# The up projections of the second model's feed-forward with seven half-size products for each two

## The chip, the core and the metric

The kernel runs on one core of a Trainium2 chip. Its time is the device time of one execution, in microseconds (us). The engines are TensorE (PE; its weight loads are a row of their own, PEld), VectorE (DVE), ScalarE (ACT), GpSimd (POOL), and SyncE (SP), which here issues DMAs. SBUF is the memory that all of them read; PSUM takes what TensorE writes.

## The reference

The program computes two models one after the other on 512 tokens of width 1024: a block with attention, a state-space mixer, memory attention and a mixture of single-neuron experts, and then two layers of a hybrid model with three branches. All is in float32. The change touches the feed-forward at the end of each of these two layers:

```python
f = jnp.square(jax.nn.relu(rmsnorm(h, norm2_g) @ w_up)) @ w_down    # w_up: 1024 x 4096, w_down: 4096 x 1024
return h + f
```

## The kernel before

Activations lie transposed: `h` is eight tiles of 128 features x 512 tokens. A weight matrix is stored so that one DMA of 512 KB brings 128 output columns with all 1024 inputs, a tile of 128 x 8 x 128. To keep float32 accuracy, every operand X of a large product is split into H, X rounded to the engine's fast float32 form, and L, the rest X - H: `split` lets ScalarE write H and VectorE write L. A product of 1024 inputs is then eight times three matmuls, wH·xH, wH·xL and wL·xH (`mm3`, lines 170 to 172), each with its own weight load of 128 x 128 and a moving operand of 512 columns.

`weight` (line 155) takes a raw buffer `wr` (three of them), issues the load on SP, and splits into `wH`, `wL` (two each). So a product's weights are split while the one before runs, and a load starts when a raw buffer has been read.

`ffn` first multiplies the eight tiles of `h` by the norm's gain and splits them (`gain_split`), while `rstd_tile` forms the tokens' scale `rs`: squares, sums over features by TensorE (line 185), an inverse square root in small VectorE steps (lines 131 to 142), a transpose (191) and a spread over partitions (196). The scale comes in only after the product. In each of four groups come eight up products (VectorE: max(ps, 0)·rs, line 1963; ScalarE: the square, line 1964; then a split, tag `y`) and eight down products that add into `h`. Just ahead of `ffn`, `run` has eight output products that add into the same `h` (line 1949).

Nobody wrote the order of instructions down: the framework plans it. It walks the program, gives each engine a list by priority and by its own guess of durations, and puts waits where a tile or a buffer has to be ready. Each engine then goes through its list in order, so an instruction that waits holds all behind it on its engine.

Of the kernel before, what the change touches and what calls it, by code (L numbers as in the profile page):

```python
# [11 lines left out]
F32 = mybir.dt.float32  # L12
F32R = mybir.dt.float32r
I32 = mybir.dt.int32
U32 = mybir.dt.uint32
AF = mybir.ActivationFunctionType
OP = mybir.AluOpType
# [4 lines left out]
P = 128  # L22
T = 512
EPS = 1e-6
# [25 lines left out]
class Builder:  # L50
# [5 lines left out]
    def __init__(self, tc, d, ctx):  # L56
        self.tc, self.nc, self.d = tc, tc.nc, d
        self.n = 0
        self.home = {}

        self.rush = False
        self.turn, self.three = 0, True
        self.sb = ctx.enter_context(tc.tile_pool(name="sb", bufs=1))
        self.pp = ctx.enter_context(tc.tile_pool(name="pp", bufs=1, space=PSUM))
        self.dr = ctx.enter_context(tc.tile_pool(name="dr", bufs=1, space=DRAM))
        self.consts()
# [94 lines left out]
            self.split(r, H, L)  # L161
        return H, L

    def mm3(self, ps, wH, wL, xs, start=True, stop=True):

        nc = self.nc
        n = len(xs)
        for k, (xH, xL) in enumerate(xs):
            s, e = start and k == 0, stop and k == n - 1
            nc.tensor.matmul(ps, wH[:, k], xH, start=s, stop=False)  # L170
            nc.tensor.matmul(ps, wH[:, k], xL, start=False, stop=False)  # L171
            nc.tensor.matmul(ps, wL[:, k], xH, start=False, stop=e)  # L172

    def gemm(self, ap, xs, n=T, ps=None):

        H, L = ap if isinstance(ap, tuple) else self.weight(ap, len(xs))
        ps = self.psg()[:, :n] if ps is None else ps
        self.mm3(ps, H, L, xs)
        return ps


    def colsum(self, ps, acc, n=T):
# [43 lines left out]

    def rstd_tile(self, srcs, width, eps=EPS, out=None):

        acc = self.sumsq(srcs)
        cs, ps = self.pss(), self.pss()  # L230
        self.colsum(cs, acc)
        r = self.small([P, T // P])
        self.rsqrt(r, cs[:, :T // P], 1.0 / width, eps)
        self.rowbc(ps, r)
        out = acc if out is None else out
        self.nc.scalar.copy(out, ps)
        return out
# [663 lines left out]
def vcol(vec, base, n):  # L901
    return [vec[:, base + k:base + k + 1] for k in range(n)]
# [344 lines left out]
N1, CB, SN, QN, KN, GN, N2, DS, CW, GW = 0, 8, 20, 28, 32, 34, 35, 43, 51, 99  # L1247
# [56 lines left out]
        v.tensor_copy(self.cos, c)  # L1304


class Layer:
    def __init__(self, B, S, l, pool):
        self.B, self.S, self.l, self.pool = B, S, l, pool
# [575 lines left out]
    def run(self, h, hpool, new_h):  # L1885

        B, nc, tc = self.B, self.B.nc, self.B.tc
        v = nc.vector

        g = vcol(self.vec, N1, 8)  # L1890
        xr = B.gain_split(h, g, lambda: B.hl("y"))
        rs = B.rstd_tile(h, 1024)
        xs = B.norm_split(h, g, 1024, "x", rs=rs)
# [24 lines left out]
        with tc.tile_pool(name=f"gdn{self.l}", bufs=1) as pool:  # L1918
# [3 lines left out]
            for n in range(8):  # L1922
                m = []
                for b in range(2):
                    o, q = B.wg(), B.wg()
# [7 lines left out]
        h, hpool = new_h()  # L1933
        mixed = []
        for n in range(8):
            g, m, o = B.wg(), B.wg(), B.wg()
# [3 lines left out]
            ps = B.gemm(B.d["w_o2"][self.l, 2, n], ys)  # L1940
            v.scalar_tensor_tensor(o, g, 1.0, ps, op0=OP.add, op1=OP.mult)
            v.tensor_tensor(o, o, m, op=OP.add)
            H, L = B.hl("x")
            nc.scalar.activation(H, o, AF.Copy, scale=0.5)
            v.scalar_tensor_tensor(L, o, 0.5, f32(H), op0=OP.mult, op1=OP.subtract)
            mixed.append((H, L))
        for n in range(8):
            ps = B.gemm(B.d["w_o2"][self.l, 3, n], mixed)
            v.tensor_tensor(h[n], h[n], ps, op=OP.add)
        self.ffn(h)  # L1950
        return h, hpool

    def ffn(self, h):

        B, nc = self.B, self.B.nc
        xs = B.gain_split(h, vcol(self.vec, N2, 8), lambda: B.hl("x"))
        rs = B.rstd_tile(h, 1024)
        for g in range(4):
            fs = []
            for c in range(8):  # L1960
                ps = B.gemm(B.d["w_up2"][self.l, 8 * g + c], xs)
                r, f = B.wg(), B.wg()
                nc.vector.scalar_tensor_tensor(r, ps, 0.0, rs, op0=OP.max, op1=OP.mult)
                nc.scalar.activation(f, r, AF.Square)
                H, L = B.hl("y")
                B.split(f, H, L)
                fs.append((H, L))
            for n in range(8):
                ps = B.gemm(B.d["w_dn2"][self.l, g, n], fs)
                nc.vector.tensor_tensor(h[n], h[n], ps, op=OP.add)  # L1970
# [53 lines left out]
```

## Time and profile before

| | before |
|---|---|
| median of three runs | 4667.72 us (4659.89 to 4668.2) |
| profiled execution | 4666.07 us, its span 4664.4 us |
| TensorE / VectorE / ScalarE / GpSimd busy | 98% / 61% / 41% / 1% |
| matmuls | 22121 |
| up products of both layers | 64, each 24 matmuls of 512 columns |

Busy time counts an instruction from start to end, and instructions of one engine overlap at their edges, so a matmul of 0.4 us does not cost 0.4 us: what counts is the distance from one start to the next.

### The profile page before, as it was taken

The numbers are of one execution on the slowest core, as the hardware profiler recorded it, in microseconds if no ns is written. First come the engines' busy times: TensorE is split into PE (matmuls) and PEld (weight loads), VectorE is DVE, ScalarE is ACT, GpSimd is POOL, SyncE is SP. The second block draws the span as 40 slices with busy tenths as digits, with TensorE's granted clock in tenths as the row PEclk, the third lists the DMA queues.
The fourth block names the chain that finished last, engine by engine and source line by source line (L and its number), as shares of the span: only waits on it lengthen the run. The fifth ranks groups of instructions, "written<-read, shape, count | busy, mean of one in ns | idle before, by whom it ended". The sixth has DMA issues, their size and how long they took to land.

```text
span 4664.4 us, 59083 instructions
## 1 busy us (share of the span) xinstructions
PE 4566.1 (98%) x22121; PEld 3668.7 (79%) x22121; DVE 2850.5 (61%) x5795; ACT 1911.1 (41%) x3695; POOL 29.6 (1%) x61
## 2 busy tenths in 40 slices
PE   8899999999999999999999999999999999999998
PEld 6777888888888888887787688888877876888887
DVE  8856898665555455556887544544488865545434
ACT  3544367863332222323553533333255534333322
POOL 0100000000000000000000000000000000000000
PEclk9899999999999999999999999999999999999999
DMA  4332245564444344442354255433324533543332
GB/s 135 92 105 68 79 148 190 183 212 127 139 144 139 122 127 138 143 138 71 98 178 139 64 162 162 147 95 95 102 85 140 177 99 95 161 158 127 95 95 81
DMA packets 306046, 589.24 MB, mean 126 GB/s; under 512 B 60192, under 2 KB 147552, under 8 KB 303584
## 3 DMA queue, kind: packets, MB, share of 16 engines
q1 hardware_dynamic: 304480, 582.88, 38.6%
q0 software_dynamic: 1280, 2.59, 0.3%
q8 instruction: 174, 2.85, 0.3%
q14 instruction: 112, 0.92, 0.1%
HBM read 480.29 MB, written 105.09 MB: 125 GB/s over the span
## 4 chain that ended last, share of the span: by engine, by line
PE 83%; DVE 7%; DMA 3%; ACT 1%; issue 1%; SPq 0%; DVEq 0%; ACTq 0%
PE g L171 13%; PE g L170 13%; PE g L172 13%; PE o L170 6%; PE o L171 6%; PE o L172 6%; PE s L1213 5%; PE s L1214 5%; PE s L1212 4%; PE s L1159 3%; DVE wL L149 2%; PE s L265 1%; DMA vr<-in_pv 1%; DMA ga<-ad 1%; PE s L1634 1%
## 5 line engine op out<-in xcount | busy, mean ns | idle before, releaser
L148 ACT ACTIVATE wH<-wr 128x1024 fp32r<-128x1024 f32 (+2 forms) x599 | 603.5, 1007 | 1303.1 <-PE g L171 790.3
L149 DVE TENSOR_TENSOR wL<-wr,wH 128x1024 fp32r<-128x1024 f32 (+2 forms) x599 | 692.2, 1156 | 439.2 <-ACT wH L148 425.4
L170 PE MATMUL g<-xH,wH 128*128 128x512 f32 (+1 forms) x2328 | 919.6, 395 | 24.7 <-ACT wH L148 12.8
L172 PE MATMUL g<-xH,wL 128*128 128x512 f32 (+1 forms) x2328 | 916.7, 394 | 5.2 <-DVE wL L149 5.2
L171 PE MATMUL g<-xL,wH 128*128 128x512 f32 (+1 forms) x2328 | 921.1, 396 | 0.3 <-DVE xL L149 0.3
L170 PEld LDWEIGHTS g<-xH,wH 128*128 128x128 f32 x2328 | 442.4, 190 | 120.3 <-issue 12.8
L172 PEld LDWEIGHTS g<-xH,wL 128*128 128x128 f32 x2328 | 442.6, 190 | 101.9 <-DVE wL L149 8.6
L171 PEld LDWEIGHTS g<-xL,wH 128*128 128x128 f32 x2328 | 442.7, 190 | 94.6 <-issue 1.9
L170 PE MATMUL o<-xH,wH 128*128 128x512 f32 x1032 | 412.4, 400 | 6.4 <-ACT w L704 4.8
L172 PE MATMUL o<-xH,wL 128*128 128x512 f32 x1032 | 412.4, 400 | 1.7 <-DVE wL L149 1.7
L171 PE MATMUL o<-xL,wH 128*128 128x512 f32 x1032 | 412.5, 400 | 0.0
L1213 PE MATMUL s<-WL,VH 128*128 128x512 f32 x1024 | 400.3, 391 | 3.7 <-DVE WL L149 3.4
L1212 PE MATMUL s<-WH,VH 128*128 128x512 f32 x1024 | 398.3, 391 | 0.5 <-ACT WH L148 0.4
L1214 PE MATMUL s<-WH,VL 128*128 128x512 f32 x1024 | 397.7, 390 | 0.0
L148 ACT ACTIVATE VH<-vr 128x1024 fp32r<-128x1024 f32 x128 | 132.4, 1056 | 537.1 <-PE s L1213 378.4
L1215 DVE TENSOR_TENSOR h<-h,s 128x512 f32<-128x512 f32 x256 | 173.4, 685 | 258.3 <-PE s L1214 258.1
L172 PE MATMUL g<-yH,wL 128*128 128x512 f32 x632 | 250.9, 397 | 1.6 <-DVE wL L149 1.6
L171 PE MATMUL g<-yL,wH 128*128 128x512 f32 x632 | 250.8, 397 | 0.3 <-DVE yL L246 0.3
L170 PE MATMUL g<-yH,wH 128*128 128x512 f32 x632 | 251.0, 397 | 0.0
L149 DVE TENSOR_TENSOR VL<-vr,VH 128x1024 fp32r<-128x1024 f32 x128 | 154.1, 1223 | 148.3 <-ACT VH L148 148.0
L170 PEld LDWEIGHTS o<-xH,wH 128*128 128x128 f32 x1032 | 194.9, 189 | 49.6 <-ACT w L704 4.9
L172 PEld LDWEIGHTS o<-xH,wL 128*128 128x128 f32 x1032 | 194.8, 189 | 46.2 <-DVE wL L149 2.6
(645 smaller groups left out, 7031.6 us busy)
## 6 DMA issues: line engine op xcount, KB each, us to landing
wr<-in_w_in SPq DMA_DIRECT2D x166, 512.0 KB, 3.6
wr<-in_pu SPq DMA_DIRECT2D x128, 512.0 KB, 4.2
vr<-in_pv SPq DMA_DIRECT2D x128, 512.0 KB, 3.6
gd<-G SPq DMA_DIRECT2D x16, 2048.0 KB, 6.5
gt<-gd SPq DMA_DIRECT2D x64, 512.0 KB, 5.8
wr<-in_w_o SPq DMA_DIRECT2D x64, 512.0 KB, 3.6
wr<-in_w_up SPq DMA_DIRECT2D x64, 512.0 KB, 3.5
wr<-in_w_dn SPq DMA_DIRECT2D x64, 512.0 KB, 3.5
```

What stands on the lines that cost most here:

```text
L148: nc.scalar.activation(H, src, AF.Copy)
L149: nc.vector.tensor_tensor(L, src, f32(H), op=OP.subtract)
L170: nc.tensor.matmul(ps, wH[:, k], xH, start=s, stop=False)
L171: nc.tensor.matmul(ps, wH[:, k], xL, start=False, stop=False)
L172: nc.tensor.matmul(ps, wL[:, k], xH, start=False, stop=e)
L265: self.nc.tensor.transpose(ps[:, tb * P:(tb + 1) * P], src[:, tb * P:(tb + 1) * P], self.ident)
L1159: nc.tensor.matmul(ps[:, j * P:(j + 1) * P], o2[:, k], og[:, j], start=True, stop=True)
L1212: nc.tensor.matmul(ps, VH[:, n], WH, start=k == 0, stop=False)
L1213: nc.tensor.matmul(ps, VH[:, n], WL, start=False, stop=False)
L1214: nc.tensor.matmul(ps, VL[:, n], WH, start=False, stop=k == 3)
L1215: nc.vector.tensor_tensor(h[n], h[n], ps, op=OP.add)
L1634: nc.tensor.matmul(ps[:, k * P:], vt[h][:, k * P:(k + 1) * P], pTs[h][k], start=k == 0, stop=k == 3)
```

## The change

Two up tiles (256 output columns) are now one 2 x 2 block product: weights a11, a12 (first and last 512 inputs of the first tile), a21, a22 (of the second), and the moving side r1, r2 (first and last four k tiles) in two halves of 256 tokens each. Eight half-size products would be the plain way; Winograd's form of Strassen's scheme takes seven, with sums of weights s1 to s4, sums of moving halves t1 to t4, and sums of results.

- `fast_weights` loads the two raw tiles, forms s1 = a21 + a22, s2 = s1 - a11, s3 = a11 - a21, s4 = a12 - s2 on GpSimd (128 x 512 each), and splits seven halves of 128 x 512 in four parts: (a11, s1), (s2, a12), (s3, s4), (a22). Parts go in turn into tags `w` and `v`, two buffers each; the raw tiles still have three.
- `fast_moving` forms t1 to t4 on VectorE and splits them, once per layer, during the output products, whose order is now `HALVES` so that tiles k and k + 4 come together.
- `fast_gemm` runs the seven products in three PSUM banks x, y, z. Products 1, 3, 5, 7 add up in x, and after 1, 3 and 5 ScalarE copies x out (u0, u1, u2). Product 4 is in z; 2 and 6 add up in y, and between these two VectorE must have read y for c2 = y + u2. c1 = z + u0 beside y + u1; the rest of c2 is x itself.
- The first pair's weights are begun ahead of the output products, in tags `v`, `v`, `w`, `w`. The tags `x` and `y` of moving and result splits are exchanged. The scale is formed after the first pair's products.

Each of its product calls is 12 matmuls of 256 columns. The diff, cut to its core:

```diff
+    def fast_moving(self, raws, main, extra):
+        v, n = self.nc.vector, T // 2
+        forms = [[] for _ in range(7)]
+        raws = iter(raws)
+        for k in range(4):
+            r1, r2 = next(raws), next(raws)
+            t = self.w2(), self.w2()
+            t1, t2, t3, t4 = t[0][:, :n], t[0][:, n:], t[1][:, :n], t[1][:, n:]
+            v.tensor_tensor(t1, r1[:, n:], r1[:, :n], op=OP.subtract)
+            v.tensor_tensor(t3, r2[:, n:], r1[:, n:], op=OP.subtract)
+            v.tensor_tensor(t2, r2[:, n:], t1, op=OP.subtract)
+            v.tensor_tensor(t4, r2[:, :n], t2, op=OP.subtract)
+            A, Bt, E = main(), main(), extra()
+            for src, (H, L) in ((r1[:, :n], [x[:, :n] for x in A]), (t1, [x[:, n:] for x in A]),
+                                (t2, [x[:, :n] for x in E]), (r2, Bt), (t[1], [x[:, n:] for x in E])):
+                self.split(src, H, L)
+            two = lambda p, o: tuple(x[:, o:o + n] for x in p)
+            for f, x in zip(forms, (two(A, 0), two(Bt, 0), two(Bt, n), two(E, 2 * n), two(A, n),
+                                    two(E, 0), two(E, n))):
+                f.append(x)
+        next(raws, None)
+        return forms
+    def fast_weights(self, ap1, ap2, pool, homes="wvwv"):
+        nc, v = self.nc, self.nc.vector
+        r = []
+        for ap in (ap1, ap2):
+            r.append(self.t([P, 8, P], F32, "wr", 3))
+            nc.sync.dma_start(r[-1], ap)
+        a11, a12, a21, a22 = r[0][:, :4], r[0][:, 4:], r[1][:, :4], r[1][:, 4:]
+        s = [self.w2().rearrange("p (k m) -> p k m", k=4) for _ in range(4)]
+        s1, s2, s3, s4 = s
+        def parts(i, *srcs):
+            tag, home = homes[i], pool if homes[i] == "v" else None
+            H, L = (self.t([P, 8, P], F32R, tag + k, 2, home) for k in "HL")
+            out = []
+            for i, src in enumerate(srcs):
+                sl = slice(4 * i, 4 * i + 4)
+                self.split(src, H[:, sl], L[:, sl])
+                out.append((H[:, sl], L[:, sl]))
+            return out
+        nc.gpsimd.tensor_tensor(s1, a21, a22, op=OP.add)
+        yield parts(0, a11, s1)
+        nc.gpsimd.tensor_tensor(s2, s1, a11, op=OP.subtract)
+        yield parts(1, s2, a12)
+        nc.gpsimd.tensor_tensor(s3, a11, a21, op=OP.subtract)
+        nc.gpsimd.tensor_tensor(s4, a12, s2, op=OP.subtract)
+        yield parts(2, s3, s4)
+        yield parts(3, a22)
+    def fast_gemm(self, w, forms, part, tile):
+        nc, v, n = self.nc, self.nc.vector, T // 2
+        x, y, z = self.pss()[:, :n], self.pss()[:, :n], self.psg()[:, :n]
+        c1, c2 = tile(), tile()
+        u = part(), part(), part()
+        def product(ps, wt, form, start):
+            self.mm3(ps, *wt, form, start=start, skip_group_check=True)
+        a, b = next(w)
+        product(x, a, forms[0], True)
+        nc.scalar.copy(u[0], x)
+        product(y, b, forms[4], True)
+        a, b = next(w)
+        product(x, a, forms[5], False)
+        nc.scalar.copy(u[1], x)
+        product(z, b, forms[1], True)
+        v.tensor_tensor(c1[:, :n], z, u[0], op=OP.add)
+        a, b = next(w)
+        product(x, a, forms[6], False)
+        nc.scalar.copy(u[2], x)
+        v.tensor_tensor(c2[:, n:], y, u[2], op=OP.add)
+        (c,) = next(w)
+        product(y, b, forms[2], False)
+        v.tensor_tensor(c1[:, n:], y, u[1], op=OP.add)
+        product(x, c, forms[3], False)
+        return c1, (x, c2)
...
+HALVES = (0, 4, 1, 5, 2, 6, 3, 7)
...
-        for n in range(8):
+        fpool = ExitStack()
+        pool = fpool.enter_context(tc.tile_pool(name=f"ffn{self.l}", bufs=1))
+        def up(c, **more):
+            return B.fast_weights(*(B.d["w_up2"][self.l, c + i] for i in range(2)), pool, **more)
+        first = up(0, homes="vvww")
+        begun = chain([next(first), next(first)], first)
+        for n in HALVES:
             ps = B.gemm(B.d["w_o2"][self.l, 3, n], mixed)
             v.tensor_tensor(h[n], h[n], ps, op=OP.add)
-        self.ffn(h)
+        self.ffn(h, pool, up, begun)
+        fpool.close()
         return h, hpool
-    def ffn(self, h):
+    def ffn(self, h, pool, up, begun):
         B, nc = self.B, self.B.nc
-        xs = B.gain_split(h, vcol(self.vec, N2, 8), lambda: B.hl("x"))
-        rs = B.rstd_tile(h, 1024)
+        g8 = vcol(self.vec, N2, 8)
+        half = T // 2
+        acc = B.t([P, T], F32, "acc", 1)
+        def raws():
+            for k in HALVES:
+                r = B.w2()
+                nc.scalar.activation(r, h[k], AF.Copy, scale=g8[k])
+                yield r
+                q = B.w2() if k else acc
+                nc.scalar.activation(q, h[k], AF.Square)
+                if k:
+                    nc.vector.tensor_tensor(acc, acc, q, op=OP.add)
+        forms = B.fast_moving(raws(), lambda: B.hl("y"),
+                              lambda: [B.t([P, 3 * half], F32R, "xt" + k, 4, pool) for k in "HL"])
+        rs = None
         for g in range(4):
             fs = []
-            for c in range(8):
-                ps = B.gemm(B.d["w_up2"][self.l, 8 * g + c], xs)
-                r, f = B.wg(), B.wg()
-                nc.vector.scalar_tensor_tensor(r, ps, 0.0, rs, op0=OP.max, op1=OP.mult)
-                nc.scalar.activation(f, r, AF.Square)
-                H, L = B.hl("y")
-                B.split(f, H, L)
-                fs.append((H, L))
+            for c in range(0, 8, 2):
+                w = up(8 * g + c) if g + c else begun
+                c1, (x, c2) = B.fast_gemm(w, forms, lambda: B.t([P, half], F32, "fu", 3, pool), B.wg)
+                if rs is None:
+                    rs = B.rstd_of(acc, 1024, first=True)
+                for out, ps, sl in ((c1, c1, slice(0, T)), (c2, x, slice(0, half)),
+                                    (c2, c2[:, half:], slice(half, T))):
+                    nc.vector.scalar_tensor_tensor(out[:, sl], ps, 0.0, rs[:, sl], op0=OP.max, op1=OP.mult)
+                for r in (c1, c2):
+                    f = B.wg()
+                    nc.scalar.activation(f, r, AF.Square)
+                    H, L = B.hl("x")
+                    B.split(f, H, L)
+                    fs.append((H, L))
             for n in range(8):
                 ps = B.gemm(B.d["w_dn2"][self.l, g, n], fs)
                 nc.vector.tensor_tensor(h[n], h[n], ps, op=OP.add)
```

How the plan changes, at three places. On TensorE, in the second group of layer 0, where the first pair ends and the second begins. Before, a product's 24 rows stood in one piece, of this form (out o, moving x, weights w; two of the eight k tiles shown):

```order
L170 MATMUL o_26410<-xH_26233,wH_26406 128x512
L171 MATMUL o_26410<-xL_26234,wH_26406 128x512
L172 MATMUL o_26410<-xH_26233,wL_26407 128x512
L170 MATMUL o_26410<-xH_26237,wH_26406 128x512
L171 MATMUL o_26410<-xL_26238,wH_26406 128x512
L172 MATMUL o_26410<-xH_26237,wL_26407 128x512
```

Now (s_27245 is x of the first pair, s_27246 its y, s_27392 x of the second pair):

```order
L172 MATMUL s_27245<-xtH_26370,wL_27329 128x256
L170 MATMUL s_27392<-yH_26270,wH_27409 128x256
...
L170 MATMUL s_27392<-yH_26302,wH_27409 128x256
L170 MATMUL s_27245<-xtH_26274,vH_27348 128x256
...
L171 MATMUL s_27245<-xtL_26307,vH_27348 128x256
L170 MATMUL s_27246<-yH_26272,wH_27328 128x256
...
L172 MATMUL s_27246<-yH_26368,wL_27329 128x256
L172 MATMUL s_27245<-xtH_26306,vL_27349 128x256
```

Behind product 5's last row stand four matmuls of the next pair's product 1, five of product 7, then product 6 whole, and the rest of 7: nine matmuls between 5 and 6.

On VectorE, in the up products. Before, one product's share (scaled result, weights of the product after, split of the square):

```order
L1963 SCALAR_TENSOR_TENSOR wg_27493<-o_27468,acc_26265 128x512
L149 TENSOR_TENSOR wL_27543<-wr_27540,wH_27542 128x1024
L149 TENSOR_TENSOR yL_27498<-wg_27494,yH_27497 128x512
L1963 SCALAR_TENSOR_TENSOR wg_27532<-g_27507,acc_26265 128x512
L149 TENSOR_TENSOR wL_27582<-wr_27579,wH_27581 128x1024
L149 TENSOR_TENSOR yL_27537<-wg_27533,yH_27536 128x512
```

Now, the second pair of that group with the third pair's weights (wr_27547 and wr_27549 are that pair's raw tiles, w_6079 its s1, w_6080 s2, w_6081 s3, w_6082 s4; fu is a copy u; s_27392 and s_27393 are x and y):

```order
L149 TENSOR_TENSOR wL_27557<-wr_27547,wH_27556 128x512
L149 TENSOR_TENSOR wL_27557<-w_6079_27551,wH_27556 128x512
L266 TENSOR_TENSOR wg_27395<-g_27394,fu_27397 128x256
L149 TENSOR_TENSOR vL_27589<-w_6080_27552,vH_27588 128x512
L149 TENSOR_TENSOR vL_27589<-wr_27547,vH_27588 128x512
L270 TENSOR_TENSOR wg_27396<-s_27393,fu_27399 128x256
L2097 SCALAR_TENSOR_TENSOR wg_27396<-wg_27396,acc_26258 128x256
L273 TENSOR_TENSOR wg_27395<-s_27393,fu_27398 128x256
L2097 SCALAR_TENSOR_TENSOR wg_27395<-wg_27395,acc_26258 128x512
L2097 SCALAR_TENSOR_TENSOR wg_27396<-s_27392,acc_26258 128x256
L149 TENSOR_TENSOR wL_27623<-w_6081_27553,wH_27622 128x512
L149 TENSOR_TENSOR wL_27623<-w_6082_27554,wH_27622 128x512
```

Three more rows end the pair's turn: the split of a22 and two splits of squares. Row L270 (c2), for which product 6 waits, stands behind four weight splits of the next pair.

On ScalarE, before, two rows of results to one of weights:

```order
L148 ACTIVATE wH_27542<-wr_27540 128x1024
L1964 ACTIVATE wg_27494<-wg_27493 128x512
L148 ACTIVATE yH_27497<-wg_27494 128x512
L148 ACTIVATE wH_27581<-wr_27579 128x1024
L1964 ACTIVATE wg_27533<-wg_27532 128x512
```

Now, from the second pair's s3 and s4 (w_6053, w_6054) to its copies u0, u1 (L260, L264):

```order
L148 ACTIVATE wH_27475<-w_6053_27406 128x512
L148 ACTIVATE wH_27475<-w_6054_27407 128x512
L148 ACTIVATE vH_27495<-wr_27402 128x512
L2100 ACTIVATE wg_27380<-wg_27248 128x512
L2100 ACTIVATE wg_27386<-wg_27249 128x512
L148 ACTIVATE xH_27382<-wg_27380 128x512
L148 ACTIVATE xH_27388<-wg_27386 128x512
L260 COPY fu_27397<-s_27392 128x256
L148 ACTIVATE wH_27556<-wr_27547 128x512
L148 ACTIVATE wH_27556<-w_6079_27551 128x512
L264 COPY fu_27398<-s_27392 128x256
```

The copy u0 of a pair now stands behind seven rows of 128x512: the pair's own s3, s4 and a22, and the squares and splits of the pair before.

## Rows read from the trace of the kernel before

**Rows 1.** The page's head: span, and busy time of each engine.

```profile
span 4664.4 us, 59083 instructions
PE 4566.1 (98%) x22121; PEld 3668.7 (79%) x22121; DVE 2850.5 (61%) x5795; ACT 1911.1 (41%) x3695; POOL 29.6 (1%) x61
```

**Rows 2.** Busy time by stretch: memory stage, up and down products of layer 0.

```profile
core 0: us, PE busy (x) PEld busy (x) DVE busy (x) ACT busy (x) POOL busy (x), PEclk, DMA share, GB/s
205.90:208.90 3.00, 3.00 (x27) 3.00 (x27) 2.99 (x7) 0.72 (x3) 0.00 (x0) 1.00 0.24 46
3110.00:3165.00 55.00, 55.00 (x239) 44.58 (x238) 21.86 (x25) 15.66 (x21) 0.00 (x0) 1.00 0.31 96
```

**Rows 3.** Timeline, start and length in us: first and last of 23 matmuls.

```profile
206.21 0.28 PE L171 MATMUL g<-xL,wH 128*128 128x256 f32 x1
...
208.82 0.28 PE L172 MATMUL g<-xH,wL 128*128 128x256 f32 x1
```

**Rows 4.** Timeline: an up product's last matmul, and its reader.

```profile
3064.34 0.40 PE L172 MATMUL g<-xH,wL 128*128 128x512 f32 x1
...
3064.78 0.69 DVE L1963 SCALAR_TENSOR_TENSOR wg<-g,acc 128x512 f32<-128x512 f32 x1 [2.82 <-PE g L172]
```

**Rows 5.** Timeline of ScalarE in the up products.

```profile
3054.55 0.61 ACT L148 ACTIVATE yH<-wg 128x512 fp32r<-128x512 f32 x1
3055.07 0.62 ACT L1964 ACTIVATE wg<-wg 128x512 f32<-128x512 f32 x1
3055.72 0.63 ACT L148 ACTIVATE yH<-wg 128x512 fp32r<-128x512 f32 x1
```

**Rows 6.** One line's instructions (ns min/median/max): a copy of 256 columns from PSUM.

```profile
L953 ACT COPY mk<-g x8: 350/353/372, 189.1 to 216.8; 128x256 f32<-128x256 f32 x8
```

**Rows 7.** Timeline of VectorE: neighbours of 256 and of 512 columns.

```profile
200.44 0.42 DVE L669 TENSOR_TENSOR s5t<-w,roti 128x256 f32<-128x256 f32 x1
200.79 0.42 DVE L668 TENSOR_TENSOR s5t<-w,rotr 128x256 f32<-128x256 f32 x1
...
205.33 0.68 DVE L495 TENSOR_TENSOR s5t<-bbr,pwi 128x512 f32<-128x512 f32 x1
205.94 0.68 DVE L493 TENSOR_TENSOR gr<-s5t,s5t 128x512 f32<-128x512 f32 x1
```

**Rows 8.** Groups by form (busy us, mean ns, idle before): splits, layer 0's feed-forward.

```profile
L149 DVE TENSOR_TENSOR wL<-wr,wH 128x1024 fp32r<-128x1024 f32 x65 | 79.6, 1225 | 11.7 <-ACT wH L148 11.7
L149 DVE TENSOR_TENSOR yL<-wg,yH 128x512 fp32r<-128x512 f32 x32 | 22.1, 692 | 0.0
```

**Rows 9.** Groups by form of GpSimd, whole program.

```profile
L1666 POOL TENSOR_SCALAR_AFFINE_SELECT blkT<-blkT 128x1024 f32<-128x1024 f32 x2 | 2.5, 1267 | 2542.0 <-PE g L172 1299.3 <-DVE blkT L1665 1242.7
L839 POOL MEMSET w<- 128x512 f32 x4 | 2.2, 558 | 54.1 <-DVE qk L844 25.4 <-DVE acc L212 17.1 <-PE s L830 11.5
...
L109 POOL TENSOR_SCALAR_AFFINE_SELECT ident<-ones 128x128 f32<-128x128 f32 x1 | 0.3, 291 | 0.6 <-DVE ones L106 0.6
```

**Rows 10.** Timeline: GpSimd and VectorE at the same time, two places.

```profile
992.62 1.23 DVE L149 TENSOR_TENSOR wL<-wr,wH 128x1024 fp32r<-128x1024 f32 x1 [4.37 <-ACT wH L148]
993.16 0.83 POOL L1262 TENSOR_SCALAR_AFFINE_SELECT low<-ones 128x128 f32<-128x128 f32 x1 [220.93 <-ACT ga L1167]
...
2295.10 1.26 POOL L1666 TENSOR_SCALAR_AFFINE_SELECT blkT<-blkT 128x1024 f32<-128x1024 f32 x1 [1299.27 <-PE g L172]
2295.80 1.63 DVE L149 TENSOR_TENSOR wL<-wr,wH 128x1024 fp32r<-128x1024 f32 x1 [0.90 <-ACT wH L148]
```

**Rows 11.** One line's instructions: all weight splits (ns min/median/max).

```profile
L149 DVE TENSOR_TENSOR wL<-wr,wH x599: 424/1225/1629, 12.8 to 4636.7; 128x1024 fp32r<-128x1024 f32 x180, 128x512 fp32r<-128x512 f32 x10, 128x256 fp32r<-128x256 f32 x10
```

**Rows 12.** DMA issues: count, KB each, median us to landing.

```profile
wr<-in_w_up SPq DMA_DIRECT2D x64, 512.0 KB, 3.5
```

**Rows 13.** Timeline: the scale's chain at the opening of layer 0's feed-forward.

```profile
3044.95 0.95 PE L185 MATMUL s<-ones,acc 128*128 128x1 f32 x8
...
3051.72 0.59 ACT L236 COPY acc<-s 128x512 f32<-128x512 f32 x1 [1.06 <-PE s L196]
```

**Rows 14.** TensorE's waits: us in total, times, longest.

```profile
PE g L170 <- DVE wg L1338: 9.8, 3, 3.9
```

More of the change, by code (lines that the diff above doesn't have):

```diff
@@ L162, in weight, with mm3 @@
         return H, L
-    def mm3(self, ps, wH, wL, xs, start=True, stop=True):
+    def mm3(self, ps, wH, wL, xs, start=True, stop=True, **more):
         nc = self.nc
@@ L169, in mm3 @@
             s, e = start and k == 0, stop and k == n - 1
-            nc.tensor.matmul(ps, wH[:, k], xH, start=s, stop=False)
-            nc.tensor.matmul(ps, wH[:, k], xL, start=False, stop=False)
-            nc.tensor.matmul(ps, wL[:, k], xH, start=False, stop=e)
+            nc.tensor.matmul(ps, wH[:, k], xH, start=s, stop=False, **more)
+            nc.tensor.matmul(ps, wH[:, k], xL, start=False, stop=False, **more)
+            nc.tensor.matmul(ps, wL[:, k], xH, start=False, stop=e, **more)
     def gemm(self, ap, xs, n=T, ps=None):
@@ L227, in rstd_tile, with rstd_of @@
     def rstd_tile(self, srcs, width, eps=EPS, out=None):
-        acc = self.sumsq(srcs)
+        return self.rstd_of(self.sumsq(srcs), width, eps, out)
+    def rstd_of(self, acc, width, eps=EPS, out=None, first=False):
         cs, ps = self.pss(), self.pss()
@@ L232, in rstd_tile @@
         r = self.small([P, T // P])
-        self.rsqrt(r, cs[:, :T // P], 1.0 / width, eps)
+        with self.tc.high_priority() if first else nullcontext():
+            self.rsqrt(r, cs[:, :T // P], 1.0 / width, eps)
         self.rowbc(ps, r)
```

## The prediction

> **What bounds the kernel now.** I read the page's head first, then stretches, then single rows. TensorE is busy 98% of 4664.4 us, VectorE 61%, ScalarE 41%, GpSimd 1% [rows 1]. In the stage that the change rewrites TensorE never waits: 55.00 us of 55.00 busy, while VectorE is busy 21.86 us and ScalarE 15.66 us [rows 2]. So this stage costs what its matmuls cost, and two engines have room beside them. 239 matmuls of 512 columns in 55.00 us is 0.230 us each, so a product of 24 takes 5.52 us. All 64 up products (32 per layer) take 353 us.
>
> **Term 1, the products.** For each pair of up products there were 48 matmuls of 512 columns, 11.05 us. Now there are 7 x 12 = 84 of 256 columns. The trace has such matmuls in the memory stage: from 206.21 to 208.82 lie 22 steps, 0.1186 us each [rows 3], a little more than half of 0.230, with the weight load busy 3.00 of 3.00 us beside them [rows 2]. 84 x 0.1186 = 9.96 us, 1.09 us less. 32 pairs: **-34.7 us**. The arithmetic saving of one eighth would be 44; a tenth of a matmul's step does not halve. The program gains 1153 matmul rows, and 32 x 84 - 64 x 24 is 1152, so the change does what it says.
>
> **Term 2, ScalarE's ring.** VectorE and ScalarE get more to do per pair. ScalarE: seven half-weight copies, two squares, two splits of 128x512, and three copies of 128x256. A 128x512 step lasts 0.61 to 0.63 us, but the next one starts after 0.52 [rows 5]; I count 0.53. The copy of 256 columns is 0.35 [rows 6]. That is 11 x 0.53 + 3 x 0.35 = 6.9 us of 9.96, which fits in sum. In order it fits less well. The copies of s3 and s4 may start only when the sixth product of the pair before is over, since they reuse its buffers. Behind them on ScalarE stand a22, two squares, two splits, and only then the copy u0, for which the third product of the next pair waits (the order rows of the change show this chain). From the start of the sixth product's last matmul: 0.28 for its end [rows 3] and 0.04 to the reader [rows 4], 7 x 0.53 = 3.71, 0.35 for u0, 0.05 back to TensorE: 4.43 us. From the third product to the sixth product's last matmul lie 50 steps, 5.93 us. The ring takes 10.36 us against 9.96, so I take 0.4 us of waiting per pair: 32 x 0.4 = **+12.8 us**. Bounds: 0 if the squares move into gaps, 0.8 if the short wait for u2 (0.13 us before the seventh product goes on, four matmuls being too few to cover 0.72 us) and for c2 add to it.
>
> **Term 3, the sums on GpSimd.** VectorE's share per pair: nine splits and two scalings of two SBUF inputs, and four operations that read PSUM. A 128x512 step lasts 0.68 to 0.69 us and starts 0.61 us after the one before, one of 256 columns 0.35 after [rows 7, 8]: nearly 8 us of 10. By itself that fits. GpSimd adds four TENSOR_TENSOR of 128x512 per pair, which the trace has nowhere. The nearest rows: a MEMSET of 128x512, 0.56 us, that reads nothing, and an AFFINE_SELECT of 128x1024, 1.27 us [rows 9]. A sum reads two streams of 512, so I take 1.27; the ends are 0.56 and 2.53 (one AFFINE_SELECT for each input).
>
> What decides is whether both engines can work at once. Two places of the trace say no. At 2295.80 a weight split of 128x1024 starts while GpSimd's AFFINE_SELECT runs from 2295.10 to 2296.36. It takes 1.63 us, the longest of 599 whose median is 1.225, and ends 1.07 us after the AFFINE_SELECT [rows 10, 11]; 0.53 us per 512 elements. It moved nothing until GpSimd was done. At 993.16 it is the other way round: an AFFINE_SELECT of 128x128, 0.29 us elsewhere [rows 9], takes 0.83, and ends 0.14 us after the weight split that began before it (992.62 + 1.23 = 993.85) [rows 10]. A MEMSET on GpSimd, which reads nothing, kept 0.56 us on the mean [rows 9].
>
> [...]
>
> Where the two collide: a pair's second raw tile takes the buffer of the first raw tile of the pair before, whose last reader is the VectorE split of a12, just ahead of c2 = y + u2. From there SP issues the load and it lands 3.5 us later [rows 12]. Then GpSimd's four sums start, while VectorE has nine splits of two SBUF inputs to do before the next split of a12, and behind that stands c2, for which the sixth product waits. If the engines take turns, that stretch is 3.55 + 9 splits (four at 0.53, their start hidden behind the lock, five at 0.61) 5.2 + four sums less their hidden start (1.27 - 0.15) 4.5 + 0.35 for c1 = 13.6 us, 3.2 above the ring's 10.4. If VectorE goes first and only s1 and s2 must stand ahead, it is 3.55 + 5.5 + 2.2 + 0.35 = 11.6, 1.2 above. I take the middle, 2.2, as nothing shows who is next. Not every pair pays. In each group of four the first pair's sums lie beside the down products of the group before, and the second's beside the first pair with three microseconds of slack; the fourth pair prepares no other. Two of four, 16 of 32: **+35 us** (19 to 51).
>
> **Term 4, the openings.** In each layer the moving sums now stand between the last output products and the first up products: fifteen steps of VectorE, nearly 9 us, beside each 11.1 us of TensorE. The halves are formed in an order that follows the output products, so most is covered. The chain for the scale (128x1 sums at 3044.95 to the copy at 3051.72 [rows 13]) was covered by products of 5.5 us; now TensorE meets its transpose some 91 short matmuls, 10.8 us, after the opening, with weight splits and GpSimd's sums mixed into VectorE's small steps. I take 3 us per layer, 0 to 7.4 (the chain in the open, 6.8 and its last copy 0.59): **+6 us**.
>
> **Taken at nothing.** SP issues the same 64 loads of 512 KB, in pairs; their landing of 3.5 us is inside term 3. GpSimd's queue has no DMA in this part of the program, so nothing stands behind a waiting sum but the next sum. Layer 1's other stages come out in another order; the matmuls are the same. The largest waits of this kind are 9.8 us in three places [rows 14], so I allow 10 us either way.
>
> **Sum.** -34.7 + 12.8 + 35 + 6 = +19 us on the profiled run's 4666.07 us, which is 1.65 us under the median of the three runs: 4685 us. With the terms' ends, not all at once: 4668 to 4706. A difference under 0.2% (9.3 us) can't be told from none here.
>
> **Rivals.**
> - No collision: sums of GpSimd and VectorE's splits run side by side, as the profile's busy shares invite one to think. Place: the two middle pairs of each group. Price: term 3 is 0 and the openings are 4, so -34.7 + 12.8 + 4 = -18: 4648 us, 4635 if ScalarE's ring is hidden too. It decides once term 3 falls under 1.0 us per touched pair ((34.7 - 12.8 - 6) / 16). For it: single-engine sums fit. Against: the two stretched rows [rows 10]. Chance 0.27.
> - [...] Chance 0.2.
> - Turns, as forecast: 4685 us. Chance 0.45.
> - A sum takes 2.53 us: the stretch is 3.55 + 5.2 + 9.6 + 0.35 = 18.7, 8.3 above the ring, so 133 instead of 35: 4783 us. Against: 1.27 us was enough for 1024 elements. Chance 0.06.
> - The short matmuls don't come at 0.119 us with the second halves as operands, and the stage is no shorter at all: some 35 us more. Chance 0.02.
>
> Faster by over 0.2%: 0.28; within it: 0.2; slower: 0.52. The range must reach to the first rival, so 4640 to 4712.
>
> **What would show it.** Term 1: rows of 128x256 at steps of 0.119 us. Term 2: TensorE's waits name the copy u0 of ScalarE. Term 3: VectorE's 128x512 splits in the up stage have a mean well above 0.69 us, their longest near 1.9, GpSimd's sums spread likewise, and TensorE waits for c2 before the sixth product, in the second and third pair of a group above all; first and fourth pairs take about 10.4 us, those 12 to 13.6. If splits keep 0.69 us beside running sums, term 3 is wrong and the change is faster. If all pairs take 10.4 us although splits stretch, the slack was larger than I worked out.

## The result, and the profile after

The changed kernel takes 4722.88 us (median of four runs, 4718.34 to 4726.38), the kernel before 4664.33 us beside it: a ratio of 1.0124, 95% interval [1.0109, 1.0139]. It is slower by 58.6 us. The forecast was slower by 19, with a range that ended at 4712. The direction and the main mechanism held, the size did not.

The page's head of the changed kernel, the answer to [rows 1]:

```profile
span 4716.6 us, 62299 instructions
PE 4568.6 (97%) x23273; PEld 3720.3 (79%) x23273; DVE 3074.6 (65%) x6139; ACT 2008.7 (43%) x3991; POOL 238.1 (5%) x189
```

TensorE's busy time did not fall, although an eighth of the up products' multiplications went: in the two feed-forwards (with the output products ahead of them) it is busy for 397.8 of 423.5 and 397.9 of 423.9 us, before for 397.9 of 397.9 and 398.9 of 398.9. What the products saved is lost again inside the busy time, where some steps are slower (sized in the section on the prediction), and the waits come on top. The short matmuls themselves run as forecast where nothing holds them up. Here are the first and the last of 43 rows in a stretch without a wait (start and length in us): 42 steps in 4.98 us, 0.1186 us each, as in [rows 3].

```profile
3158.87 0.28 PE L172 MATMUL s<-yH,wL 128*128 128x256 f32 x1
...
3163.85 0.29 PE L172 MATMUL g<-yH,vL 128*128 128x256 f32 x1
```

But the stretches are short. Busy time in 50 us of up products of layer 0, beside [rows 2]:

```profile
3155.00:3205.00 50.00, 44.73 (x319) 41.42 (x318) 39.10 (x54) 24.82 (x48) 14.00 (x9) 0.97 0.29 85
```

TensorE, which never waited here, is idle for 5.3 us of 50, and VectorE rose from 40% to 78%. TensorE's waits (total us, times, longest) say for whom:

```profile
PE s L172 <- DVE wL L149: 23.4, 16, 3.1
PE s L170 <- DVE wg L270: 20.3, 19, 1.8
...
PE s L170 <- ACT fu L260: 0.5, 1, 0.5
```

Weight splits (L149) and c2 = y + u2 (L270), both VectorE's. The copy u0 on ScalarE (L260), which the forecast's second term named, is waited for once (a wait is counted from 0.15 us on).

Now the two engines that share the work. First GpSimd's sums (busy us, mean ns), then VectorE's operations of the same line by form (ns min/median/max):

```profile
L239 POOL TENSOR_TENSOR w<-w,wr 128x512 f32<-128x512 f32 x32 | 55.4, 1732 | 2.5
...
L237 POOL TENSOR_TENSOR w<-wr 128x512 f32<-128x512 f32 x32 | 48.8, 1525 | 1825.4 <-DVE wg L2044 1379.3 <-DMA wr<-in_w_up 426.0 <-DVE wg L273 14.2
```

```profile
L149 DVE TENSOR_TENSOR wL<-w,wH x94: 676/686/1796, 3055.0 to 4646.3; 128x512 fp32r<-128x512 f32 x94
...
L149 DVE TENSOR_TENSOR xL<-wg,xH x64: 677/692/1780, 3075.0 to 4658.3; 128x512 fp32r<-128x512 f32 x64
...
L2097 DVE SCALAR_TENSOR_TENSOR wg<-s,acc x32: 410/419/425, 3073.0 to 4655.8; 128x256 f32<-128x256 f32 x32
```

A split of two SBUF inputs takes up to 1.80 us, 1.1 more than its median. The operation with one input in PSUM (s) stays within 0.41 and 0.43. The timeline of one pair's sums (GpSimd's rows, then VectorE's in the same time) shows why:

```profile
3256.02 1.79 POOL L237 TENSOR_TENSOR w<-wr 128x512 f32<-128x512 f32 x1 [5.65 <-DMA wr<-in_w_up]
3257.89 1.62 POOL L239 TENSOR_TENSOR w<-w,wr 128x512 f32<-128x512 f32 x1
3259.48 1.73 POOL L241 TENSOR_TENSOR w<-wr,wr 128x512 f32<-128x512 f32 x1
3261.17 1.73 POOL L242 TENSOR_TENSOR w<-wr,w 128x512 f32<-128x512 f32 x1
```

```profile
3255.97 2.39 DVE L149 TENSOR_TENSOR wL<-w,wH 128x512 fp32r<-128x512 f32 x2
3258.28 1.77 DVE L149 TENSOR_TENSOR vL<-wr,vH 128x512 fp32r<-128x512 f32 x1
3259.98 3.47 DVE L149 TENSOR_TENSOR xL<-wg,xH 128x512 fp32r<-128x512 f32 x2
3263.37 0.68 DVE L149 TENSOR_TENSOR wL<-wr,wH 128x512 fp32r<-128x512 f32 x1
...
3264.58 0.41 DVE L266 TENSOR_TENSOR wg<-g,fu 128x256 f32<-128x256 f32 x1
3264.91 0.68 DVE L149 TENSOR_TENSOR vL<-w,vH 128x512 fp32r<-128x512 f32 x1
3265.51 0.68 DVE L149 TENSOR_TENSOR vL<-wr,vH 128x512 fp32r<-128x512 f32 x1
3266.11 0.41 DVE L270 TENSOR_TENSOR wg<-s,fu 128x256 f32<-128x256 f32 x1
```

The engines take turns: one split, one sum, one split, one sum, at 1.7 us a round, where a split beside no sum takes 0.68 us and a sum that met nothing 1.29. In what follows this is called the lock. Five splits took 7.4 us in place of 3.1. As soon as the fourth sum is over (3262.90), the splits are back at 0.68. Then c2 has to wait for its place behind four weight splits, and TensorE for c2. The distance from one c2 to the next, read so in the second to fourth groups of both layers (the later groups), is 13.7 to 14.7 us for the second and third pair of a group and 10.5 for the fourth, once 11.6. The sums of a group's first pair lie beside the down products and cost TensorE nothing there (in the second to fourth groups of layer 0 it is busy for all 6.6 to 6.8 us that those four sums take).

Of the 128 sums one had to wait for more than one operation. It is the first sum of layer 0's opening (GpSimd's row, then VectorE's):

```profile
3053.50 3.92 POOL L237 TENSOR_TENSOR w<-wr 128x512 f32<-128x512 f32 x1 [3.95 <-DMA wr<-in_w_up]
```

```profile
3053.46 1.02 DVE L149 TENSOR_TENSOR xtL<-w,xtH 128x256 fp32r<-128x256 f32 x2
3054.39 0.69 DVE L2083 TENSOR_TENSOR acc<-acc,w 128x512 f32<-128x512 f32 x1
3054.99 1.29 DVE L149 TENSOR_TENSOR wL<-w,wH 128x512 fp32r<-128x512 f32 x2
```

There VectorE went through five operations at its usual pace, and the sum got on only when VectorE had none left. Why it lost its turn there and nowhere else is not shown.

In the opening of layer 0 the same lock meets three of the small steps of the tokens' scale, 0.16 to 0.17 us each without it; in layer 1 it meets none, and all twelve take 0.15 to 0.16. The rows of layer 0:

```profile
3057.97 1.23 DVE L135 TENSOR_SCALAR sm<-sm 128x4 int32<-128x4 int32 x1
3059.12 0.68 DVE L149 TENSOR_TENSOR vL<-wr,vH 128x512 fp32r<-128x512 f32 x1
3059.72 1.25 DVE L138 TENSOR_TENSOR sm<-sm 128x4 f32<-128x4 f32 x1
3061.00 1.19 DVE L140 SCALAR_TENSOR_TENSOR sm<-sm,sm 128x4 f32<-128x4 f32 x1
```

### The profile page after: what moved, and what is told of

Same layout as the page of the kernel before. It is cut to its first block, busy times and chain, and to the rows that moved or that the text cites. A ratio compares the mean times of both kernels' runs of the same rounds, so it can differ in the third digit from the quotient of the medians.

```text
span 4716.6 us, 62299 instructions
## 1 busy us (share of the span) xinstructions
PE 4568.6 (97%) x23273; PEld 3720.3 (79%) x23273; DVE 3074.6 (65%) x6139; ACT 2008.7 (43%) x3991; POOL 238.1 (5%) x189
## 4 chain that ended last, share of the span: by engine, by line
PE 77%; DVE 12%; DMA 3%; ACT 2%; issue 1%; SPq 0%; DVEq 0%; ACTq 0%
PE g L171 11%; PE g L172 11%; PE g L170 11%; PE o L170 5%; PE o L171 5%; PE o L172 5%; PE s L1312 5%; PE s L1313 5%; PE s L1311 5%; DVE wL L149 3%; PE s L1258 3%; PE s L170 1%; PE s L364 1%; PE s L172 1%; PE s L171 1%
## 5 line engine op out<-in xcount | busy, mean ns | idle before, releaser
L148 ACT ACTIVATE wH<-wr 128x1024 fp32r<-128x1024 f32 (+2 forms) x567 | 555.6, 980 | 1014.6 <-PE g L171 584.0
L149 DVE TENSOR_TENSOR wL<-wr,wH 128x1024 fp32r<-128x1024 f32 (+2 forms) x567 | 648.1, 1143 | 445.6 <-ACT wH L148 425.5
L172 PEld LDWEIGHTS g<-xH,wL 128*128 128x128 f32 x2312 | 439.0, 190 | 103.6 <-DVE wL L149 11.8
L171 PEld LDWEIGHTS g<-xL,wH 128*128 128x128 f32 x2312 | 439.0, 190 | 95.3 <-issue 2.3
L149 DVE TENSOR_TENSOR VL<-vr,VH 128x1024 fp32r<-128x1024 f32 x128 | 154.1, 1224 | 145.3 <-ACT VH L148 145.1
L171 PEld LDWEIGHTS o<-xL,wH 128*128 128x128 f32 x1048 | 198.7, 190 | 44.4 <-issue 0.2
L1312 PEld LDWEIGHTS s<-WL,VH 128*128 128x128 f32 x1024 | 192.2, 188 | 48.9 <-DVE WL L149 9.3
L1311 PEld LDWEIGHTS s<-WH,VH 128*128 128x128 f32 x1024 | 191.9, 188 | 45.6 <-ACT WH L148 4.3
```

Source lines behind the costliest of these rows:

```text
L148: nc.scalar.activation(H, src, AF.Copy)
L149: nc.vector.tensor_tensor(L, src, f32(H), op=OP.subtract)
L171: nc.tensor.matmul(ps, wH[:, k], xL, start=False, stop=False, **more)
L172: nc.tensor.matmul(ps, wL[:, k], xH, start=False, stop=e, **more)
L1311: nc.tensor.matmul(ps, VH[:, n], WH, start=k == 0, stop=False)
L1312: nc.tensor.matmul(ps, VH[:, n], WL, start=False, stop=False)
```

## The experiments

All times are medians, each with its ratio to the kernel before on the same chip.

**1. The sums on VectorE.**

```diff
-        nc.gpsimd.tensor_tensor(s1, a21, a22, op=OP.add)
+        v.tensor_tensor(s1, a21, a22, op=OP.add)
...      (s2, s3, s4 likewise)
```

> The four weight sums of each pair run on VectorE instead of GpSimd, nothing else. Lock theory (a GpSimd sum holds VectorE off for about 1.1 us, four of them 4.4 us in each pair whose sums fall among VectorE's splits, two pairs of four): VectorE gets 4 x 0.61 = 2.4 us of work in place of 4.4 us of standing still, so the pairs that took 13.7 to 14.6 us take some 12, and the time falls by about 16 x 2 = 32 us, to 4690 (4678 to 4702). Rival, no lock (VectorE is simply full, or its order is bad): 2.4 us more of work per pair, the time rises by 16 x 2.4 = 39 us, to 4760.

Measured: 4637.58 us, ratio 0.9939 [0.9922, 0.9955]. No pair in a later group takes over 10.9 us. The rival "VectorE is simply full" falls: 128 more operations on VectorE made the kernel 85 us faster than the change. The lock theory's direction holds, but its 4690 was 52 too high; pairs of 12 us were expected. The timeline of VectorE shows one reason: two sums stand where VectorE would have waited for the sixth product, between c2 (L270) and y + u1 (L273), and cost nothing there.

```profile
3235.68 0.42 DVE L270 TENSOR_TENSOR wg<-s,fu 128x256 f32<-128x256 f32 x1
3236.02 0.68 DVE L241 TENSOR_TENSOR w<-wr,wr 128x512 f32<-128x512 f32 x1
...
3236.95 0.68 DVE L242 TENSOR_TENSOR w<-wr,w 128x512 f32<-128x512 f32 x1
3238.04 0.42 DVE L273 TENSOR_TENSOR wg<-s,fu 128x256 f32<-128x256 f32 x1 [0.40 <-PE s L172]
```

The other reason is that I had counted nothing for the openings beyond 2 us for each touched pair, and the first groups shorten by 10 us each (60.7 to 50.5); the eighth experiment sizes them. Some 8 us more are scatter: by so much the changed kernel's profiled run is behind this one's already at the first output product of layer 0, ahead of the change. This version beats both kernels.

**2. Memsets in place of the sums.**

```diff
-        nc.gpsimd.tensor_tensor(s1, a21, a22, op=OP.add)
+        nc.gpsimd.memset(s1, 1.0)
...      (s2, s3, s4 likewise)
```

> Each of the four weight sums is replaced by a GpSimd memset of the same tile, which reads nothing, so the weight sums are left out of the computation. Same engine, same splits, same number of instructions; the memset also need not wait for the raw weights. Lock theory: VectorE's splits keep 0.69 us at the longest, and no pair takes over 10.6 us: 8 groups x 7 us = 56 and some 8 us in the two openings come back, to 4659 (4650 to 4670). Rival, order (the sum c2 = y + u2 is late because it stands behind four weight splits on VectorE, and TensorE waits for it whatever GpSimd does): pairs stay at 13 us or more, 4710 to 4725.

Measured: 4637.74 us, ratio 0.9941 [0.9924, 0.9958]. The longest split beside GpSimd's 128 memsets:

```profile
L149 DVE TENSOR_TENSOR wL<-w,wH x94: 680/684/693, 3043.1 to 4562.3; 128x512 fp32r<-128x512 f32 x94
```

0.693 in place of 1.796. Pairs of the later groups take 10.6 us each, so c2's place in the order alone costs nearly nothing, and that rival falls. A memset is also shorter than a sum (0.53 us) and doesn't wait for the raw weights, so this run doesn't yet tell the lock from sums that come late; experiment 5 does. 4659 was too high by 21. Between the two profiled runs lie 84 us: 45 in the later groups (42 expected), 27 in the first groups and output products (22 expected), and 12 outside these stages, 10 of them ahead of layer 0's output products. So half of the miss has nothing to do with the change.

**3 and 4. c2 ahead of the splits**, with the sums on GpSimd, and with the sums on VectorE.

```diff
-                self.split(src, H[:, sl], L[:, sl])
+                with self.tc.issue_after(self.c2) if homes == "wvwv" and home else nullcontext():
+                    self.split(src, H[:, sl], L[:, sl])
...
-        v.tensor_tensor(c2[:, n:], y, u[2], op=OP.add)
+        self.c2 = v.tensor_tensor(c2[:, n:], y, u[2], op=OP.add).ins
```

> The sums stay on GpSimd; VectorE's splits of the next pair's second part (s2 and a12) and of a22 are kept behind c2 = y + u2, for which the sixth product waits. Both theories give something: VectorE stands idle for some 1.3 us after c2 until the sixth product is done, and can do the two splits there. Lock theory with a ring through VectorE: 1.2 us less in each of 16 pairs, about 20 us, to 4703 (4695 to 4713), and the splits are still stretched to 1.8 us. Order as the whole cause: all of the 58 us comes back but the openings, 4675 or below. If the wait for the weights' splits decides instead, nothing changes: 4723.

> Both edits: the sums on VectorE and c2 ahead of the splits. Lock theory: the two gains add up as long as VectorE bounds the pair (32 + 20): about 4671 (4660 to 4685), about level with the kernel before the change. Rival, no lock: 4760 less at most 20, 4740.

Measured: 4689.56 us, ratio 1.0049 [1.0032, 1.0065], and 4639.66 us, 0.9943 [0.9926, 0.9959]. With the lock the better order gives 33 us back (20 expected): the second and third pairs of the later groups take 11.8 to 13.6 us. 4689.56 lies under the expected range, which began at 4695. Without the lock it gives nothing (2 us slower, less than can be told). So the order only says how much of the lock TensorE sees; the gains do not add up, as I had expected them to, and 4671 was 31 too high.

**5. Sums that nobody reads.** Experiment 1, and behind each sum an addition on GpSimd into a tile without a reader.

```diff
+        junk = self.t([P, 4, 112], F32, "junk", 1, pool)
+        again = lambda x: nc.gpsimd.tensor_tensor(junk, x[:, :, :112], x[:, :, 16:], op=OP.add)
         v.tensor_tensor(s1, a21, a22, op=OP.add)
+        again(s1)
...      (s2, s3, s4 likewise)
```

> The sums stay on VectorE as in the first experiment, and GpSimd forms after each of them one addition of two SBUF inputs (448 columns) that nothing reads. VectorE's order is the same row for row. Lock theory: although no result of GpSimd is waited for, VectorE stands still for 4 x 0.95 us in each pair whose additions fall among its splits, so a pair takes 8.1 + 2.4 + 3.8 = 14.3 us in place of 10.2: 16 x 4.1 = 66 us in the steady pairs and 10 to 20 in the openings, to 4710 (4690 to 4740), and two-input operations of VectorE are stretched to 1.6 us or more while those with an input in PSUM keep 0.42 and 0.69 us. Rival, lateness (GpSimd's sums cost because they are slow and come late to the splits that need them, 1.3 us against 0.6): nobody needs these, the time stays 4638.

Measured: 4717.16 us, ratio 1.0113 [1.0096, 1.013]. Nearly the whole loss is back (80 of 85 us), though VectorE's order is that of experiment 1 and no result of GpSimd is used. No engine waits for GpSimd in these two feed-forwards. The rival, that the sums come late, falls. Two forms of VectorE in this run, with two inputs in SBUF and with one in PSUM (s):

```profile
L149 DVE TENSOR_TENSOR wL<-w,wH x94: 674/679/1647, 3048.8 to 4640.9; 128x512 fp32r<-128x512 f32 x94
```

```profile
L276 DVE TENSOR_TENSOR wg<-s,fu x32: 409/412/426, 3052.4 to 4645.0; 128x256 f32<-128x256 f32 x32
```

The expected sizes hold: up to 1.65 us for the first, 0.43 for the second. From one group's first down product to the next group's it takes 93.6 to 95.2 us here, 93.4 to 95.3 in the change and 85.6 to 85.8 in experiment 1, so a later group loses 8.4 us to sums that nobody reads; two pairs of 4.1 were expected. Which pairs lose was not as I had it: the second to fourth take 10.3 to 13.3 us, 4 us a group more than in experiment 1, and the other half falls to the first pair. (VectorE's last three additions into h come up to 8.7 us apart in this run, behind the sums of the next pair. TensorE loses nothing by that, as its busy time in such a stretch shows:)

```profile
3126.00:3142.00 16.00, 16.00 (x71) 12.86 (x70) 12.96 (x14) 4.78 (x7) 5.61 (x4) 1.00 0.26 71
```

**6. Two sums on each engine**: s1 and s2 on VectorE, edited as in experiment 1, s3 and s4 on GpSimd.

> s1 and s2 on VectorE, s3 and s4 on GpSimd as in the change. Lock theory, VectorE at its limit: a touched pair takes 8.1 + 2 x 0.61 + 2 x 1.08 = 11.5 us against 10.2 with all four on VectorE and 13.7 to 14.6 with all four on GpSimd: 16 x 1.3 = 21 us and some 8 us in the openings more than 4638, so 4667 (4650 to 4680). Rival, lateness of s1 and s2, which stand first in a pair: with these on VectorE the loss is gone, 4640.

Measured: 4662.42 us, ratio 0.9993 [0.9983, 1.0003]: no difference from the kernel before. Half the sums on GpSimd cost 25 us, the other half 60 more. That fits a price that rises once VectorE has no room left; no run puts s1 and s2 alone on GpSimd, so it isn't shown that it is the number of the sums and not their place.

**7. The kernel before, with sums that nobody reads.**

```diff
             self.split(r, H, L)
+        for _ in range(2 if self.extra else 0):     # in up products only
+            junk = self.t([P, 4, P], F32, "junk", 1, self.extra)
+            nc.gpsimd.tensor_tensor(junk, r[:, :4], r[:, 4:], op=OP.add)
```

> The kernel before the change, with two additions of 128x512 on GpSimd per up product (four per pair, as many as in the change) that nothing reads. Lock theory with cover: VectorE's splits are stretched by about 1.08 us each time, up to 2.3 us for one of 1024 columns, but VectorE is busy only 21.9 of 55.0 us in this stage, and 2 x 1.08 us more for each product of 5.5 us still fits: TensorE's pace and the time stay, 4665 (4658 to 4675). Rival, the lock costs TensorE whatever room VectorE has: 64 x 2.16 = 138 us more, 4800.

Measured: 4679.91 us, ratio 1.003 [1.0019, 1.0042]. In the later groups it is as expected. The splits of this stretch of up products (mean 1.638 us; 1.226 in the kernel before), and its busy times:

```profile
L149 DVE TENSOR_TENSOR wL<-wr,wH 128x1024 fp32r<-128x1024 f32 x10 | 16.4, 1638 | 1.7 <-ACT wH L148 1.7
```

```profile
3131.00:3182.00 51.00, 51.00 (x221) 41.36 (x220) 29.28 (x26) 17.68 (x23) 22.37 (x14) 1.00 0.29 93
```

TensorE is busy 51.00 of 51.00 us, and a group takes 50.19, to a hundredth what it took before: here, where VectorE is busy 29.28 of 51.00 us, the lock costs TensorE nothing. The 15 us that I had not expected are in the openings. The output products and the first group lose 4.3 and 3.4 us in layer 0, 3.7 and 2.9 in layer 1. There the scale's chain, from its first sum over features to the copy of the scale, takes 11.0 and 10.6 us in place of 7.4, and in layer 0 TensorE waits 2.3 us for the squares that this chain starts from. Of the chain's small steps one goes from 0.16 to 1.25 us in each layer (in layer 1 another takes 1.11). The rows of layer 0:

```profile
3055.62 1.89 DVE L149 TENSOR_TENSOR wL<-wr,wH 128x1024 fp32r<-128x1024 f32 x1 [1.73 <-ACT wH L148]
3057.43 1.25 DVE L138 TENSOR_TENSOR sm<-sm 128x4 f32<-128x4 f32 x1
```

**8. Only the openings freed.** `fast_weights` takes the engine of the sums as an argument:

```diff
+            ... pool, eng=nc.vector if c < 8 else nc.gpsimd, **more)
```

> The sums of the first group of each layer (four pairs of sixteen) on VectorE, the other twelve pairs' on GpSimd as in the change. It tells what the openings' share of the loss is. Lock theory, by the group lengths of the two kernels: a first group took 60.7 us with all sums on GpSimd and 50.5 with all on VectorE, so 2 x 10.2 = 20 us come back, and one to two more in the output products: 4701 (4694 to 4708), while the second to fourth groups keep their 55 us. Rival, a loss that each pair has alike, openings no more than others: 4 pairs of 16 are a quarter of 85, 4702 less nothing for the openings themselves, but then first groups with VectorE's sums must still take some 55 us and the others fall below 55.

Measured: 4687.9 us, ratio 1.005 [1.0033, 1.0066]. The first groups take 50.5 us, the others 54.3 to 56.2, as the lock theory has it. In the traces the output products and feed-forwards of both layers shorten by some 22 us, as expected; the medians differ by 35. The median lies 6 us under the expected range (4694 to 4708). The other 13 I cannot place. The profiled run was the slowest of its four (4695.05) and the change's own the fastest of its four, so run-to-run scatter, 8 to 10 us in both kernels, is part of it.

The lengths of the groups, from the start of VectorE's last addition into h before a group's up products to its first one behind them (so eight up products and one down product), in us:

| kernel | layer 0: groups 1 to 4 | layer 1: groups 1 to 4 |
|---|---|---|
| before | 51.3, 50.2, 50.2, 50.2 | 51.4, 50.4, 50.4, 50.4 |
| after | 60.7, 55.1, 54.2, 55.4 | 60.8, 56.1, 55.8, 54.3 |
| 1, sums on VectorE | 50.5, 45.8, 46.0, 46.5 | 50.5, 46.5, 46.5, 46.2 |
| 2, memsets | 49.0, 47.6, 47.6, 47.6 | 49.0, 47.6, 47.6, 47.6 |
| 6, two and two | 53.2, 48.3, 48.4, 48.5 | 53.8, 48.4, 48.4, 48.5 |
| 8, openings freed | 50.5, 54.5, 55.5, 54.3 | 50.5, 56.2, 55.5, 54.3 |

Without a wait a group would take 4 x 9.96 + 5.6 = 45.4 (5.6 is the distance of two down products). The marks are VectorE's: in experiments 1 and 6 its last additions into h come up to 0.6 and 1.0 us late behind sums, and a group that starts there looks shorter by as much. By whole rounds, as in experiment 5, a later group of experiment 1 is 1.1 us above that floor.

## Why the prediction was wrong in size

Against the profiled runs, 4716.6 - 4664.4 = +52.2 us of span (the medians differ by 58.6; no trace shows where the other 6 lie):

- **Term 1, the products: -34.7, right.** The step is 0.1186 us, and with the sums on VectorE the later groups come within 1.1 us of their floor. Two asides beside the sum were off: 0.1186 against half of 0.230 means that 3% of a step does not halve, not a tenth, and the trace has 1152 matmuls more, not 1153.
- **Term 2, ScalarE's ring: +12.8, about right in size, by luck.** Pairs free of the lock take 10.5 (fourth pairs) to 10.6 us (experiment 2), 10.4 forecast. But TensorE names the copy u0 once in the whole run. With the sums on VectorE the fourth pairs take 9.7 to 9.9 us and all pairs of the later groups 10.24 on the mean, so a ring of 10.36 does not bind. In experiment 2 TensorE has no wait over 0.15 us in the later groups of layer 0; it loses its 0.6 us a pair in single steps of 0.22 to 0.29 us where one product follows another. What makes them is not shown.
- **Term 3, the lock: +35, mis-sized; measured about +59.** That an operation with one input in PSUM keeps its pace beside the sums, as this term takes it, stood on no row of before; in the change's trace such an operation keeps 0.41 to 0.43 us. The step that failed is "I take the middle, 2.2, as nothing shows who is next". In the up products the engines take turns, the case that the forecast had priced at its outer end. The twelve second and third pairs of the later groups sum to 168.3 us; less 12 x 10.36 that is 44.0, for six groups, and 58.7 for eight. That is 3.7 us a pair, half a microsecond above the forecast's own outer end (3.2, from a stretch of 13.6). Eight of the twelve take 13.7 to 13.8, so the stretch of strict turns was worked out almost to the point. In the pair shown above the split of a12 ends at 3252.45, the sums start 3.57 us later (3.55 in the forecast's stretch), and c2 starts 10.1 after that (10.05). The other four take 14.5 to 14.7. Which pairs pay, two of four, was right in the main, and so was the length of a sum, 1.27 taken: the sums of the trace that met nothing take 1.29 to 1.30.
- **Term 4, the openings: +6, mis-sized; measured about +14.** First groups take 60.7 and 60.8 us, 5.8 and 5.4 more than the mean of the later ones, and the output products 1.7 and 0.6 more than before. The step that failed is that I took the chain of the scale for what the openings cost. TensorE never waits for its transpose, and both layers lose alike, although the chain (first sum to end of the copy) takes 13.9 us in layer 0, with three stretched steps, and 10.9 in layer 1 without any; in experiment 1, with nothing to lock, it takes 11.2. The longest waits of the first groups, 3.1 us in each layer, are for a weight split. Most of the excess does not need the lock: experiment 1 has 4.4 and 4.1 us in its first groups and 1.4 and 0.6 in the output products, 10.5 in all, and experiment 2, without sums, about 2. So it comes with the sums on either engine; how, stays open.
- **Taken at nothing: about +2** by difference, inside the 10 that I allowed. It is 6.9 us ahead of layer 0's output products, most of it there by the 1000th matmul, less 5.3 between and behind the two feed-forwards.

-34.7 + 12.8 + 58.7 + 13.5 = 50.3. The two feed-forwards with their output products are 25.6 and 25.0 us longer, 50.6. Of the rivals, "no collision" falls. That VectorE goes first, the case at the low end of term 3, falls by the timeline of the up products, where the engines take turns at 1.7 us a round; the one sum of 3.92 us is the only place that looks like it. With term 3 at its outer end the forecast would have been 4701. The range ended at 4712 because the terms' ends were taken as not meeting (4706); all together they give 4723. Here term 3 went past its end, 51, and term 4 came close to its own, twice 7.4.

One thing that carried term 3 past its end is the clock. Behind some of its waits TensorE's granted clock drops. The busy times of 1.7 us behind two waits of 1.48 and 1.38 us:

```profile
3172.60:3174.30 1.70, 1.70 (x9) 1.70 (x9) 0.08 (x1) 0.00 (x0) 0.00 (x0) 0.50 0.74 183
```

The clock is 0.50 here, half of the 1.00 that it had in the two microseconds to 3172, in which TensorE was busy for 0.90. It does not always fall: behind waits of 1.47 and 1.38 us at 3264 and 3266 it stays at 1.00.

```profile
3267.00:3269.00 2.00, 2.00 (x19) 2.00 (x18) 0.65 (x2) 0.76 (x2) 0.00 (x0) 1.00 0.66 215
```

The changed kernel has some 112 steps of 0.21 us in rows of four to fifteen, 11 us more than at 0.1186; experiments 1 and 2 have none (mean granted clock of their profiled runs 0.991 and 0.992, of the change's 0.986). Such rows follow waits in the four pairs of 14.5 to 14.7 us and in the fourth pair of 11.6, and cost about 1 us in each. In term 3 that is about 5 of the 58.7 us; without it a touched pair would still be 3.4 us above the ring. The rest lies in the first groups. Besides, the first matmul behind many a wait or a change of product is followed by a step of 0.22: 94 single ones in the change, some 10 us. Experiment 2 has 83 of them, so they are not the lock's and belong to term 2. Nobody could have read the half clock off the stage before, which never waited.

## What to carry to other kernels

An engine with 1% busy is not free capacity if its work holds up one that you need, as GpSimd's sums held up VectorE's splits here (0.69 to 1.80 us). Before moving work to GpSimd, count VectorE's operations with two SBUF inputs that will run beside it: each GpSimd sum here took nearly its own length, 1.1 of 1.29 us, off VectorE, so moving 0.61 us of VectorE's work cost VectorE 1.1. It was harmless where VectorE had room (a later group of experiment 7 in layer 0, 50.19 us as before) and dear where TensorE waited for VectorE (the later groups of the change, 54.2 to 56.1 us in place of 50.2 to 50.4). If two mechanisms bound a cost and the trace does not say which applies, do not forecast the middle, which is the time of neither: forecast the one that the rows favour, and price the other as a rival.

## What was not expected of the hardware

- The lock follows the operands: splits and additions of two SBUF inputs (128x512) went from 0.69 to 1.8 us, operations with one input in PSUM kept 0.42 (128x256) and 0.69 us (128x512) beside running sums, and in the run with memsets no split of a memset tile or of a square (128x512) took over 0.695 us.
- Tiny operations paid the whole price too: three of VectorE's steps on 4 columns took 1.19 to 1.25 us in place of 0.16. One of them (L135, a TENSOR_SCALAR) has a single SBUF input and took 1.23 us beside a sum.
- Some waits of TensorE cost more than their length: two waits of 1.48 and 1.38 us were followed by 1.7 us at a granted clock of 0.50, two of 1.47 and 1.38 us elsewhere by 2.0 us at 1.00.
- Of the change's 128 sums 127 waited for one VectorE operation at the most; for the other, in a place where VectorE had five such operations in a row, GpSimd waited until VectorE paused.
